# Two transformer blocks on one core: token halves skewed by four weight units at the two joints with a norm over rows

## The chip, the cores and the metric

The kernel runs on one core of one Trainium2 chip. Its engines work side by side, each through its own queue in order: TensorE (PE, matrix products; PEld loads its weights), VectorE (DVE), ScalarE (ACT), GpSimd (POOL) and SyncE (SP, which issues most transfers). They wait for each other by semaphores. The metric is the device time of one execution in microseconds (us); lower is better. All values are 32-bit floating point.

## The reference, cut to what matters

256 tokens of 2048 features pass two blocks. Between the attention and the feed-forward part of the first block, and between the first and the second block, stands a norm over a token's whole row of features, and a second norm follows it at once:

```python
mixed = concat([diff_out, dsa_out]) @ w_o
x = x + gate_a * rms_norm(mixed, g_attn_post)              # joint 1
h = rms_norm(x, g_ffn_pre) * (1.0 + scale_f) + shift_f
ff = (silu(h @ w_gate) * (h @ w_up)) @ w_down
x = x + gate_f * rms_norm(ff, g_ffn_post)                  # joint 2
...
h = rms_norm(x, pre_norm_g)                                # second block
proj = h @ w_in
```

The vectors `gate_a`, `scale_f`, `shift_f`, `gate_f` come from one product of a conditioning vector with `w_ada`, whose weight tiles ("ada" items) are worked off between the other products.

## The kernel before

**Products.** The tokens are two halves of 128, t0 and t1 (t = 0, 1). A weight matrix is worked off in groups (`Grp`) of 512 columns. Its rows come in raw tiles of four chunks of 128 (`kc`), and two chunks make a *unit*. For each unit ScalarE rounds the raw weights to a high part `wh` (line 286) and VectorE subtracts it to get the low part `wl` (L287); both have four buffers. The activations have a high and a low part too (`h2h`, `h2l`, and `h3h`, `h3l`). Each chunk and half takes three products of 128 x 512 into PSUM (`mm`, L65): `wh` by high, `wl` by high, `wh` by low. So a unit is six products for one half.

**Order of the halves.** `Grp.steps()` lays a group out as a list: the first `begin` units for t0, then for t1; the units between for both halves together; the last `end` units for t0, then for t1. So t0's sum is complete `end` units before t1's. With `begin` = 2 the next group can do two units of t0 before it needs anything of t1.

**What sets the order on the engines.** The program is written out by a driver, `run`, that goes through the list of steps with a model of the clock. What follows a product (`post`) is a Python generator: at `yield d` it hands back, and the driver takes it up again when the modelled clock has gone on by d. `mark` and `done` set and ask for names such as `h2.0.0` (half 0, quarter 0). None of this waits on the chip. It decides only in which order instructions stand in the queues.

**Joint 1.** The last group of the attention's output is `wo2_3`. For each half `post_norm_in` (L1142) adds its product to `mo` on VectorE (L1145), squares on ScalarE with a sum (L1146) and multiplies by the gain (L1147). `fin_o(t)` (L1168) goes on: the root of the first norm (VectorE, POOL), then for four quarters of 512 features `resid` (L1155, VectorE: x + norm) and a square on ScalarE (L1178); the second root, put on a diagonal matrix `dg` (L1181). Then, for each quarter, four products of `xr` with `dg` on TensorE transpose and scale at once (`tp`, L65, eight records in the trace); ScalarE adds scale and shift (`hm`, L1192, four instructions); `put_split` (L1158) makes the high part (L1163 on ScalarE, or L1165, a cast on VectorE) and subtracts for the low part (L1166). There are two PSUM buffers for `tp`. `gate0`, the first group of the feed-forward part, uses h2.

**Joint 2.** `down2_3` ends the feed-forward part, `fin_f(t)` (L1261) makes h3 in the same way, with plain transposes (`tp` or `tpb`, L70) of quarters that alternate between ScalarE (L1277) and VectorE (L1273), without a second root: that follows later and is applied after the product. `qa` is the first group of the second block.

Of the kernel before, what the change touches and what calls it, by code (L numbers as in the profile page):

```python
# [39 lines left out]
def kernel(ctx: ExitStack, tc: tile.TileContext, a, freq, out):  # L40
# [32 lines left out]

    # ------------------------------------------------------------------ storage
    slots = deque(range(14))
# [20 lines left out]
    def small(n, name="sm"):  # L96
        t = smp.tile([P, 16], F32, name=name, tag="s")
        return t[:, :n]
# [22 lines left out]

    # ------------------------------------------------------------------ driver
    bg = []
# [250 lines left out]

    # ------------------------------------------------------------------ constants
    v1 = wtile(tag="P", bufs=4, name="v1")
# [129 lines left out]

    # ------------------------------------------------------------------ helpers
    def rstd_of(ssq, n, width, name="rstd"):
# [45 lines left out]

    # ------------------------------------------------------------------ modulation
    def ada_item(load, use, after=lambda: None):
# [162 lines left out]

    # ------------------------------------------------------------------ first norm  # L720
    ssx = cst.tile([P, 2, 4], F32, name="ssx")
# [29 lines left out]

    # ------------------------------------------------------------------ w_in of the first block
    acc = {}
# [43 lines left out]

    # index scores and the selection of keys
    iws = cst.tile([P, 2, 16], F32, name="iws")
# [314 lines left out]

    # ------------------------------------------------------------------ output of the attention
    mix_hi = lambda kc, t: (hid["mh%d" % (kc // 8)][:, kc % 8, t * P:(t + 1) * P],
# [51 lines left out]
    def fin_o(t):  # L1168
        while not done("ada3", "ada4"):
            yield POLL  # L1170
        if "h2" not in hid:
            hid["h2"] = mk_pair("h2")
        yield 0.5
        r = rstd_of(sum4(sso[:, t, :]), 1, D)
        s4 = small(4, "rn4")
        for q in range(4):
            xs = resid(t, q, r, mo, xr)
            A.activation(wtile(name="junk"), xs, AF.Square, accum_out=s4[:, q:q + 1])  # L1178
        r2 = rstd_of(sum4(s4), 1, D)
        dg = wtile(name="dg")[:, :P]  # L1180
        V.tensor_scalar(dg, ident, r2, None, op0=OP.mult)  # L1181
        yield 4.86
        for q in range(4):
            pb = tp_bank()
            for j in range(4):
                k = 4 * q + j
                T.matmul(pb[:, j * P:(j + 1) * P], xr[t][:, k * P:(k + 1) * P], dg, start=True, stop=True,
                         skip_group_check=True)
            m3 = wtile(name="hm").rearrange("p (c q) -> p c q", q=P)
            for j in range(4):  # L1190
                k = 4 * q + j
                A.activation(m3[:, j, :], pb[:, j * P:(j + 1) * P], AF.Identity, scale=Afcol[:, k:k + 1],  # L1192
                             bias=tfcol[:, k:k + 1])
            put_split(hid["h2"], q, t, m3, V)
            mark(f"h2.{t}.{q}")
            yield 3.07
# [5 lines left out]
    for g in range(4):  # L1202
        so2 += Grp(f"wo2_{g}", w_o, 512 * g, 512, range(0, 8), mix_hi,
                   post_norm_in(mo, sso, g, "Ga", fin_o),
                   need=lambda ks, t: ["diff", "ada2"], end=3 if g == 3 else 1).steps()
    steps += [call(mo_alloc)] + merge(so1, scale_f, 1.0)
# [5 lines left out]

    # ------------------------------------------------------------------ feed-forward
    DFF = 5632
# [46 lines left out]
    def fin_f(t):  # L1261
        if "h3" not in hid:
            free_pair("h2")
            hid["h3"] = mk_pair("h3")
        yield 0.5
        r = rstd_of(sum4(ssf[:, t, :]), 1, D)
        xs = [resid(t, q, r, ffacc, xr) for q in range(2)]
        yield 2.33
        for q in range(4):
            pb = quad_transpose(xs[q])  # L1270
            m3 = wtile(name="hm").rearrange("p (c q) -> p c q", q=P)
            if q % 2:
                V.tensor_mul(m3, pb, col1[:, 112 + 4 * q:116 + 4 * q][:, :, None].to_broadcast([P, 4, P]))  # L1273
            else:
                for j in range(4):
                    k = 4 * q + j
                    A.activation(m3[:, j, :], pb[:, j, :], AF.Copy, scale=col1[:, 112 + k:113 + k])  # L1277
            put_split(hid["h3"], q, t, m3, A)
            if q < 2:
                xs.append(resid(t, q + 2, r, ffacc, xr))  # L1280
            mark(f"h3.{t}.{q}")
            yield 1.87
        yield 7.0
        s4 = small(4, "rn4")
        for q in range(4):
            A.activation(wtile(name="junk"), xr[t][:, 512 * q:512 * (q + 1)], AF.Square,
                         accum_out=s4[:, q:q + 1])
        G.tensor_copy(r3[:, t, 0:1], rstd_of(sum4(s4), 1, D))
        V.tensor_scalar(r3[:, t, 1:2], r3[:, t, 0:1], 0.5, None, op0=OP.mult)
        park(t)  # L1290
        mark(f"r3.{t}")
# [7 lines left out]
    for p, (g0, ng) in enumerate(parts):  # L1299
        if p == 0:  # L1300
            fsteps.append(call(after_o))
        fsteps.append(call(act_alloc))
        for g in range(g0, g0 + ng):
            if g == 1:
                fsteps.append(call(rel_mo))
            for nm, w, post in (("gate", w_gate, post_gate(g)), ("up", w_up, post_up(g, g - g0))):
                fsteps += Grp(f"{nm}{g}", w, 512 * g, 512, range(16), lhs2, post,
                              need=lambda ks, t: [f"h2.{t}.{k // 4}" for k in ks],
                              begin=2 if nm + str(g) == "gate0" else 1).steps()
        for g in range(4):  # L1310
            post = post_down(g, p) if p < 2 else post_norm_in(ffacc, ssf, g, "Gf", fin_f)

            def need(ks, t, p=p, g0=g0):
                r = [f"up{k // 4}.{t}" for k in ks]
                return r + (["ada5"] if p == 2 else [])
            fsteps += Grp(f"down{p}_{g}", w_down, 512 * g, 512, range(4 * g0, 4 * (g0 + ng)), lhs_act(p),
                          post, need=need, end=3 if (p, g) == (2, 3) else 1).steps()
    nf = len(fsteps) // 4
# [3 lines left out]

    # ------------------------------------------------------------------ second block
    w_in2 = a["w_in_2"]
# [62 lines left out]

    # gated convolution
    C_IN, B_GATE, C_GATE, Z_CONV = 3136, 5184, 7232, 9280
# [79 lines left out]

    # latent attention  # L1470
    knT, vt, qnT = [None, None], [None, None], [None, None]
# [203 lines left out]

    # output projection
    ot = [None, None]
# [74 lines left out]
```

## Time and profile before

| | |
|---|---|
| runs | 2367.35, 2368.16, 2370.7 us; median 2368.16 |
| span of the profiled execution | 2365.9 us, 27898 instructions |
| TensorE busy | 2315.8 us |
| VectorE, ScalarE, GpSimd busy | 1306.1, 1069.0, 96.8 us |
| mean granted TensorE clock | 0.994 of full speed |
| data moved | 506.57 MB |

The span runs from the first to the last instruction of the one execution that was profiled; the runs are timed whole, without a profile. In a timeline a product's duration reaches past the start of the next, as products overlap: the distance of starts is the pace. Joint 1 lies between 505 and 575 us of the span, joint 2 between 1262 and 1330.

### The profile page before, as it was taken

How to read it: one execution, taken by the hardware profiler on the slowest of the kernel's cores; microseconds unless marked ns; L12 is line 12 of the kernel's file. 1: busy time of each engine (PE TensorE's matmuls, PEld its weight loads, DVE VectorE, ACT ScalarE, POOL GpSimd, SP SyncE). 2: the span in 40 equal slices, each digit the busy share in tenths (PEclk: the TensorE clock that was granted, in tenths of full speed). 3: DMA queues.
4: the chain of work that ended last, by engine and by line, in shares of the span. 5: the costliest groups of instructions: out<-in, count | busy, mean ns of one | idle time of the engine just before them, and what ended most of it. 6: DMA issues, size and time to landing. Idle time of an engine off the chain costs nothing.

```text
span 2365.9 us, 27898 instructions
## 1 busy us (share of the span) xinstructions
PE 2315.8 (98%) x11044; PEld 1842.3 (78%) x11044; DVE 1306.1 (55%) x1710; ACT 1069.0 (45%) x1503; POOL 96.8 (4%) x117
## 2 busy tenths in 40 slices
PE   7999999999999999999998999999999999999998
PEld 5666666677887888888887888888888988888887
DVE  3656756556664444554556655555544654554554
ACT  4434345546444444434444644444445544444443
POOL 1311011010000000000001000000000000000000
PEclk9999999999999999999999999999999999999999
DMA  9996888957775556556554665565565553565563
GB/s 302 330 320 237 318 309 301 318 209 277 242 261 191 191 192 195 179 196 195 186 188 144 220 195 190 179 200 188 179 204 161 168 171 125 172 219 196 187 204 125
DMA packets 237619, 506.57 MB, mean 214 GB/s; under 512 B 9288, under 2 KB 31984, under 8 KB 228400
## 3 DMA queue, kind: packets, MB, share of 16 engines
q1 hardware_dynamic: 235392, 496.14, 62.3%
q0 software_dynamic: 1872, 8.58, 1.1%
q8 instruction: 86, 1.41, 0.2%
q14 instruction: 45, 0.37, 0.0%
q10 hardware_dynamic: 224, 0.07, 0.0%
HBM read 500.56 MB, written 4.19 MB: 213 GB/s over the span
## 4 chain that ended last, share of the span: by engine, by line
PE 75%; DVE 1%; ACT 1%; issue 1%; POOL 0%; DVEq 0%; POOLq 0%; ACTq 0%
PE mm L65 71%; PE tp L70 1%; PE sc L65 1%; PE tp L65 1%; PE tpb L70 1%; DVE wl L287 0%; DVE xr L1155 0%; ACT h3h L1163 0%; DVE h3l L1166 0%; POOL rstd L513 0%; ACT wh L286 0%; ACT junk L1178 0%; DVE ot L1705 0%; ACT hm L1277 0%; DVE hm L1273 0%
## 5 line engine op out<-in xcount | busy, mean ns | idle before, releaser
L287 DVE TENSOR_TENSOR wl<-raw,wh 128x1024 fp32r<-128x1024 f32 (+3 forms) x723 | 871.9, 1212 | 766.5 <-ACT wh L286 760.4
L286 ACT ACTIVATE wh<-raw 128x1024 fp32r<-128x1024 f32 (+3 forms) x723 | 745.9, 1038 | 696.4 <-PE mm L65 686.3
L65 PE MATMUL mm<-wh,h3h 128*128 128x512 f32 (+1 forms) x992 | 387.1, 390 | 1.7 <-ACT h3h L1163 1.2
L65 PE MATMUL mm<-wl,h3h 128*128 128x512 f32 (+1 forms) x992 | 380.7, 384 | 0.4 <-DVE wl L287 0.4
L65 PE MATMUL mm<-wh,h3l 128*128 128x512 f32 (+1 forms) x992 | 381.0, 384 | 0.0
L65 PE MATMUL mm<-wh,h2h 128*128 128x512 f32 x704 | 276.3, 393 | 0.0
L65 PE MATMUL mm<-wl,h2h 128*128 128x512 f32 x704 | 274.6, 390 | 0.9 <-DVE wl L287 0.9
L65 PE MATMUL mm<-wh,h2l 128*128 128x512 f32 x704 | 274.7, 390 | 0.0
L65 PEld LDWEIGHTS mm<-wh,h3h 128*128 128x128 f32 x992 | 186.7, 188 | 37.8 <-ACT h3h L1163 1.6
L65 PEld LDWEIGHTS mm<-wh,h3l 128*128 128x128 f32 x992 | 186.5, 188 | 37.4 <-DVE h3l L1166 0.4
L65 PEld LDWEIGHTS mm<-wl,h3h 128*128 128x128 f32 x992 | 186.8, 188 | 34.8 <-DVE wl L287 0.6
L65 PE MATMUL mm<-wh,h1h 128*128 128x512 f32 (+2 forms) x384 | 154.0, 401 | 3.4 <-ACT wh L286 2.5
L65 PEld LDWEIGHTS mm<-wl,h2h 128*128 128x128 f32 x704 | 132.5, 188 | 28.1 <-DVE wl L287 1.2
L65 PEld LDWEIGHTS mm<-wh,h2h 128*128 128x128 f32 x704 | 132.5, 188 | 27.7 <-issue 0.8
L65 PEld LDWEIGHTS mm<-wh,h2l 128*128 128x128 f32 x704 | 132.4, 188 | 27.6
L65 PE MATMUL mm<-wl,h1h 128*128 128x512 f32 (+2 forms) x384 | 142.7, 372 | 7.8 <-DVE wl L287 7.8
L65 PE MATMUL mm<-wh,h1l 128*128 128x512 f32 (+2 forms) x384 | 142.0, 370 | 1.9 <-DVE h1l L627 1.9
L65 PE MATMUL mm<-wh,acth 128*128 128x512 f32 x352 | 139.3, 396 | 0.0
L65 PE MATMUL mm<-wh,actl 128*128 128x512 f32 x352 | 137.1, 390 | 0.0
L65 PE MATMUL mm<-wl,acth 128*128 128x512 f32 x352 | 137.0, 389 | 0.0
L65 PEld LDWEIGHTS mm<-wh,h1h 128*128 128x128 f32 x384 | 72.8, 190 | 55.7 <-issue 26.7
L65 PEld LDWEIGHTS mm<-wl,h1h 128*128 128x128 f32 x384 | 72.9, 190 | 21.2 <-DVE wl L287 10.9
(412 smaller groups left out, 2777.7 us busy)
## 6 DMA issues: line engine op xcount, KB each, us to landing
raw<-in_w_in_dram SPq DMA_DIRECT2D x134, 1024.0 KB, 5.2
raw<-in_w_ada_dram SPq DMA_DIRECT2D x47, 1024.0 KB, 4.9
raw<-in_w_gate_dram SPq DMA_DIRECT2D x44, 1024.0 KB, 5.3
raw<-in_w_up_dram SPq DMA_DIRECT2D x44, 1024.0 KB, 5.2
raw<-in_w_down_dram SPq DMA_DIRECT2D x44, 1024.0 KB, 5.1
raw<-in_w_ada_dram SPq DMA_DIRECT2D x36, 512.0 KB, 8.9
rawb<-in_w_ada_dram SPq DMA_DIRECT2D x17, 1024.0 KB, 6.5
raw<-in_w_o_conv_dram SPq DMA_DIRECT2D x16, 1024.0 KB, 5.1
```

What stands on the lines that cost most here:

```text
L65: return nc.tensor.matmul(o, l, r, **kw)
L70: return nc.tensor.transpose(o, i, idn)
L286: A.activation(wh[:, :m, :g.n], src, AF.Copy)
L287: V.tensor_sub(wl[:, :m, :g.n], src, wh[:, :m, :g.n])
```

## The change

`wo2_3` and `down2_3` end t0 four units before t1, not three (`wo2_3` also begins with both halves together), and `gate0` begins with four units of t0 in place of two. In `fin_o`, half t1 no longer lets time pass before its first root, and its row is written only after t0's first quarter is done; its four squares are VectorE's (new L1185) in place of ScalarE's; and the high part of h2 is ScalarE's for all quarters but the first of t0. In `fin_f`, t1 passes over the pause too, and t0's quarters 2 and 3 are written after t1's quarters 0 and 1.

```diff
@@ fin_o
-        yield 0.5
+        if t == 0:
+            yield 0.5
         r = rstd_of(sum4(sso[:, t, :]), 1, D)
         s4 = small(4, "rn4")
+        if t == 1:
+            while not done("h2.0.0"):
+                yield 0.3
         for q in range(4):
             xs = resid(t, q, r, mo, xr)
-            A.activation(wtile(name="junk"), xs, AF.Square, accum_out=s4[:, q:q + 1])
+            if t == 0:
+                A.activation(wtile(name="junk"), xs, AF.Square, accum_out=s4[:, q:q + 1])
+            else:
+                V.scalar_tensor_tensor(wtile(name="junk"), xs, 1.0, xs, op0=OP.mult, op1=OP.mult,
+                                       accum_out=s4[:, q:q + 1])
...
-            put_split(hid["h2"], q, t, m3, V)
+            put_split(hid["h2"], q, t, m3, V if t == 0 and q == 0 else A)
@@ wo2 groups
-                   need=lambda ks, t: ["diff", "ada2"], end=3 if g == 3 else 1).steps()
+                   need=lambda ks, t: ["diff", "ada2"], begin=0 if g == 3 else 1,
+                   end=4 if g == 3 else 1).steps()
@@ fin_f
-        yield 0.5
+        if t == 0:
+            yield 0.5
...
         for q in range(4):
+            if t == 0 and q >= 2:
+                while not done(f"h3.1.{q - 2}"):
+                    yield 0.3
@@ gate0
-                              begin=2 if nm + str(g) == "gate0" else 1).steps()
+                              begin=4 if nm + str(g) == "gate0" else 1).steps()
@@ down2_3
-                          post, need=need, end=3 if (p, g) == (2, 3) else 1).steps()
+                          post, need=need, end=4 if (p, g) == (2, 3) else 1).steps()
```

Three places show what moves. The first is VectorE's queue at joint 1, from the add of t1's product (`mo1`) on; `xr1` is t1's row, `dg` the diagonal, `wl` those of gate0's first two units. Before:

```order
L1145 TENSOR_TENSOR mo1_3516<-mm_4451,mo1_3516 128x512
L1147 TENSOR_TENSOR mo1_3516<-mo1_3516,Ga_3521 128x512
L518 TENSOR_REDUCE ssum_4540<-sso_274 128x1
L511 TENSOR_SCALAR rstdv_4542<-ssum_4540 128x1
L1155 SCALAR_TENSOR_TENSOR xr1_4256<-mo1_3516,rstd_4544,xr1_4256 128x512 x4
L518 TENSOR_REDUCE ssum_4559<-rn4_4546 128x1
L511 TENSOR_SCALAR rstdv_4561<-ssum_4559 128x1
L1181 TENSOR_SCALAR dg_4565<-ident_99,rstd_4563 128x128
L1165 CAST h2h0_4480<-hm_4578 128x4x128
L1166 TENSOR_TENSOR h2l0_4482<-hm_4578,h2h0_4480 128x4x128
L287 TENSOR_TENSOR wl_4592<-raw_4589,wh_4591 128x1024
L287 TENSOR_TENSOR wl_4596<-raw_4589,wh_4595 128x1024
```

and of the change:

```order
L1166 TENSOR_TENSOR h2l0_4475<-hm_4552,h2h0_4473 128x4x128
L1155 SCALAR_TENSOR_TENSOR xr1_4256<-mo1_3516,rstd_4537,xr1_4256 128x512
L1185 SCALAR_TENSOR_TENSOR junk_4560,rn4_4539<-xr1_4256 128x512
L1155 SCALAR_TENSOR_TENSOR xr1_4256<-mo1_3516,rstd_4537,xr1_4256 128x512
L1185 SCALAR_TENSOR_TENSOR junk_4563,rn4_4539<-xr1_4256 128x512
L1155 SCALAR_TENSOR_TENSOR xr1_4256<-mo1_3516,rstd_4537,xr1_4256 128x512
L1185 SCALAR_TENSOR_TENSOR junk_4566,rn4_4539<-xr1_4256 128x512
L1155 SCALAR_TENSOR_TENSOR xr1_4256<-mo1_3516,rstd_4537,xr1_4256 128x512
L1185 SCALAR_TENSOR_TENSOR junk_4569,rn4_4539<-xr1_4256 128x512
L518 TENSOR_REDUCE ssum_4571<-rn4_4539 128x1
L511 TENSOR_SCALAR rstdv_4573<-ssum_4571 128x1
L1189 TENSOR_SCALAR dg_4577<-ident_99,rstd_4575 128x128
```

The cast and subtract of t0's first quarter (the subtract is the first row here) move ahead of t1's row, and four squares (L1185) stand between the four resid and behind them, all ahead of `dg`. On TensorE the transpose of t1's first quarter, which reads that `dg`, stands ahead of gate0's first product in both kernels.

The second is ScalarE's queue at joint 1, from the transform of t0's first quarter on (`wh` first of gate0's units 0 and 1, then of unit 2, then of unit 3). Before:

```order
L1192 ACTIVATE hm_4578<-tp_4573,tfcol_130,Afcol_129 128x128 x4
L286 ACTIVATE wh_4591<-raw_4589 128x1024
L286 ACTIVATE wh_4595<-raw_4589 128x1024
L1192 ACTIVATE hm_4618<-tp_4613,tfcol_130,Afcol_129 128x128 x4
L1192 ACTIVATE hm_4630<-tp_4625,tfcol_130,Afcol_129 128x128 x4
L1192 ACTIVATE hm_4657<-tp_4652,tfcol_130,Afcol_129 128x128 x4
L1192 ACTIVATE hm_4669<-tp_4664,tfcol_130,Afcol_129 128x128 x4
L286 ACTIVATE wh_4682<-raw_4599 128x1024
L1192 ACTIVATE hm_4695<-tp_4690,tfcol_130,Afcol_129 128x128 x4
```

and of the change, from `wh` of unit 1 on:

```order
L286 ACTIVATE wh_4595<-raw_4589 128x1024
L1200 ACTIVATE hm_4612<-tp_4607,tfcol_130,Afcol_129 128x128 x4
L1163 ACTIVATE h2h0_4473<-hm_4612 128x4x128
L1200 ACTIVATE hm_4630<-tp_4625,tfcol_130,Afcol_129 128x128 x4
L1163 ACTIVATE h2h0_4473<-hm_4630 128x4x128
L1200 ACTIVATE hm_4654<-tp_4649,tfcol_130,Afcol_129 128x128 x4
L1163 ACTIVATE h2h1_4474<-hm_4654 128x4x128
L1200 ACTIVATE hm_4669<-tp_4664,tfcol_130,Afcol_129 128x128 x4
L1163 ACTIVATE h2h0_4473<-hm_4669 128x4x128
L1200 ACTIVATE hm_4684<-tp_4679,tfcol_130,Afcol_129 128x128 x4
L1163 ACTIVATE h2h1_4474<-hm_4684 128x4x128
L286 ACTIVATE wh_4694<-raw_4599 128x1024
```

Between `wh` of unit 1 and `wh` of unit 2 stood four quarters; now five stand there, each with its cast to the high part (L1163).

The third is VectorE's queue at joint 2; `ffacc1` and `xr1` are t1's, `xr0` t0's, `wl` the low parts of qa's units. Before:

```order
L287 TENSOR_TENSOR wl_9609<-raw_9444,wh_9608 128x1024
L1166 TENSOR_TENSOR h3l0_9586<-hm_9622,h3h0_9584 128x4x128
L1155 SCALAR_TENSOR_TENSOR xr0_4254<-ffacc0_4999,rstd_9595,xr0_4254 128x512
L287 TENSOR_TENSOR wl_9634<-raw_9478,wh_9633 128x1024
L1145 TENSOR_TENSOR ffacc1_5000<-mm_9517,ffacc1_5000 128x512
L1147 TENSOR_TENSOR ffacc1_5000<-ffacc1_5000,Gf_5991 128x512
L1273 TENSOR_TENSOR hm_9650<-tp_9645,col1_113 128x512
L1166 TENSOR_TENSOR h3l0_9586<-hm_9650,h3h0_9584 128x4x128
L1155 SCALAR_TENSOR_TENSOR xr0_4254<-ffacc0_4999,rstd_9595,xr0_4254 128x512
L518 TENSOR_REDUCE ssum_9655<-ssf_275 128x1
L511 TENSOR_SCALAR rstdv_9657<-ssum_9655 128x1
L1155 SCALAR_TENSOR_TENSOR xr1_4256<-ffacc1_5000,rstd_9659,xr1_4256 128x512 x2
```

and of the change:

```order
L1166 TENSOR_TENSOR h3l0_9576<-hm_9610,h3h0_9574 128x4x128
L1155 SCALAR_TENSOR_TENSOR xr0_4254<-ffacc0_5002,rstd_9585,xr0_4254 128x512
L287 TENSOR_TENSOR wl_9622<-raw_9444,wh_9621 128x1024
L1286 TENSOR_TENSOR hm_9635<-tp_9630,col1_113 128x512
L1166 TENSOR_TENSOR h3l0_9576<-hm_9635,h3h0_9574 128x4x128
L1155 SCALAR_TENSOR_TENSOR xr0_4254<-ffacc0_5002,rstd_9585,xr0_4254 128x512
L287 TENSOR_TENSOR wl_9644<-raw_9478,wh_9643 128x1024
L1145 TENSOR_TENSOR ffacc1_5003<-mm_9517,ffacc1_5003 128x512
L1147 TENSOR_TENSOR ffacc1_5003<-ffacc1_5003,Gf_5968 128x512
L518 TENSOR_REDUCE ssum_9651<-ssf_275 128x1
L511 TENSOR_SCALAR rstdv_9653<-ssum_9651 128x1
L1155 SCALAR_TENSOR_TENSOR xr1_4256<-ffacc1_5003,rstd_9655,xr1_4256 128x512 x2
```

The add of t1's product (`ffacc1<-mm`) now stands behind the transform, subtract and third resid of t0 and one more `wl`, where it stood ahead of them.

## Rows read from the trace of the kernel before

**Rows 1.** The page, part 1: busy us of each engine, share of the span, instructions

```profile
PE 2315.8 (98%) x11044; PEld 1842.3 (78%) x11044; DVE 1306.1 (55%) x1710; ACT 1069.0 (45%) x1503; POOL 96.8 (4%) x117
```

**Rows 2.** Windows, 850 to 1262: busy time and instructions by engine, clock, DMA share

```profile
850.00:1262.00 412.00, 412.00 (x1846) 341.18 (x1846) 208.87 (x190) 173.84 (x183) 5.11 (x4) 1.00 0.58 191
```

**Rows 3.** Waits of PE, 500 to 575: instruction, releaser, total, times, longest

```profile
PE tp L65 <- ACT hm L1192: 3.1, 1, 3.1
PE tp L65 <- DVE dg L1181: 2.2, 1, 2.2
PE mm L65 <- DVE wl L287: 0.9, 1, 0.9
```

**Rows 4.** Waits of PE, 1262 to 1330, the same columns

```profile
PE tpb L70 <- DVE xr L1155: 5.4, 2, 4.7
PE mm L65 <- ACT h3h L1163: 1.2, 1, 1.2
PE tp L70 <- DVE xr L1155: 0.8, 1, 0.8
```

**Rows 5.** Windows, 540 to 546, columns as in the second group

```profile
540.00:546.00 6.00, 5.30 (x20) 4.82 (x21) 5.12 (x7) 4.01 (x12) 2.22 (x5) 0.50 0.69 188
```

**Rows 6.** Timeline of PE, joint 1: start, duration, engine, line, operation [idle before]

```profile
526.31 1.92 PE L65 MATMUL ada<-raw,csil 128*32 128x512 f32 x16
530.38 1.16 PE L65 MATMUL tp<-dg,xr 128*128 128x128 f32 x8 [2.15 <-DVE dg L1181]
...
538.42 1.13 PE L65 MATMUL tp<-dg,xr 128*128 128x128 f32 x8 [3.08 <-ACT hm L1192]
...
548.54 1.95 PE L65 MATMUL tp<-dg,xr 128*128 128x128 f32 x16
...
558.76 0.39 PE L65 MATMUL mm<-wh,h2h 128*128 128x512 f32 x1
```

**Rows 7.** Timeline of DVE, joint 1

```profile
518.14 2.10 DVE L287 TENSOR_TENSOR wl<-raw,wh 128x1024 fp32r<-128x1024 f32 x1 [1.76 <-ACT wh L286]
522.34 0.69 DVE L1145 TENSOR_TENSOR mo<-mm,mo 128x512 f32<-128x512 f32 x1 [2.10 <-PE mm L65]
...
530.04 0.28 DVE L1181 TENSOR_SCALAR dg<-ident,rstd 128x128 f32<-128x128 f32 x1 [0.67 <-POOL rstd L513]
530.24 0.68 DVE L1145 TENSOR_TENSOR mo<-mm,mo 128x512 f32<-128x512 f32 x1
...
533.37 2.74 DVE L1155 SCALAR_TENSOR_TENSOR xr<-mo,rstd,xr 128x512 f32<-128x512 f32 x4 [0.65 <-POOL rstd L513]
536.96 0.16 DVE L518 TENSOR_REDUCE ssum<-rn 128x1 f32<-128x4 f32 x1 [0.85 <-ACT junk L1178]
...
538.35 0.43 DVE L1165 CAST h2h<-hm 128x512 fp32r<-128x512 f32 x1
...
539.42 2.35 DVE L287 TENSOR_TENSOR wl<-raw,wh 128x1024 fp32r<-128x1024 f32 x2
```

**Rows 8.** Timeline of ACT, joint 1

```profile
536.84 1.49 ACT L1192 ACTIVATE hm<-tp,tfcol,Afcol 128x128 f32<-128x128 f32 x4
```

**Rows 9.** Line 735, first norm: minimum, median, maximum ns; first and last start

```profile
L735 DVE SCALAR_TENSOR_TENSOR junk<-x x4: 680/684/686, 16.8 to 18.6; 128x512 f32<-128x512 f32 x4
L735 DVE DVE_READ_ACCUMULATOR junk<-x x4: 79/80/81, 17.4 to 19.2; 128x1 f32 x4
```

**Rows 10.** Timeline of ACT, joint 2

```profile
1300.28 1.12 ACT L1277 ACTIVATE hm<-tpb,col 128x128 f32<-128x128 f32 x4
...
1303.42 0.63 ACT L1163 ACTIVATE h3h<-hm 128x512 fp32r<-128x512 f32 x1 [1.36 <-DVE hm L1273]
1303.96 2.94 ACT L286 ACTIVATE wh<-raw 128x1024 fp32r<-128x1024 f32 x3
```

**Rows 11.** Timeline of DVE, joint 2

```profile
1286.25 0.68 DVE L1145 TENSOR_TENSOR ffacc<-mm,ffacc 128x512 f32<-128x512 f32 x1
...
1291.97 1.42 DVE L1155 SCALAR_TENSOR_TENSOR xr<-ffacc,rstd,xr 128x512 f32<-128x512 f32 x2 [0.66 <-POOL rstd L513]
```

## The prediction

> **What bounds the kernel now.** I read the page first: TensorE is busy for 98% of the span [rows 1], so time is won only where TensorE stands still or runs at half clock, and every microsecond added to its row of work is added to the end. A stretch far from the joints has no idle time: 1846 matrix products in 412.00 us, 0.223 us each [rows 2]. So the waits of TensorE around the two joints come next. At joint 1 they are 3.1, 2.2 and 0.9 us [rows 3], 6.2 in all; at joint 2 5.4 (two waits, the longer 4.7), 1.2 and 0.8 [rows 4], 7.4. After the first joint's the clock pays as well: its mean was 0.50, the lower of its two levels (1.2 of 2.4 GHz), over the six microseconds 540 to 546 [rows 5]. Six microseconds at 0.50 do three microseconds' work. All that the change could win back is thus some 6 + 3 us at joint 1 and 7 at joint 2.
>
> The timelines say what is waited for. At joint 1 token half t0 has its last sum added at 522.34 and its diagonal `dg` at 530.04 + 0.28 = 530.32; TensorE transposes at 530.38 [rows 6, 7]. Half t1's `dg` ends at 538.32, and its first quarter is transposed at 538.42, ahead of every product of gate0. The waits list calls that a wait for `hm`, which also ended then, at 536.84 + 1.49 = 538.33 [rows 8]: two releasers at the same instant, so moving ScalarE's work alone wins nothing.
>
> **The change, joint 1.** Times are on the clock of the trace of before.
>
> *t0 earlier.* wo2_3 now ends t0 four units before the group's end instead of three, so one unit of t1 less precedes it: six products, 6 x 0.223 = 1.3 us. But the last low part `wl` ends at 518.14 + 2.10 = 520.24 [rows 7], some 0.5 later than t0's last unit would then want it. So I take 0.9 of 1.3: add at 521.5, `dg` of t0 at 529.5, transposes at once. TensorE meanwhile has 8 instead of 16 ada products (half of 1.92 us [rows 6]) in front of them.
>
> *t1 later.* In the order, VectorE does the cast and subtract of t0's first quarter before t1's row. ScalarE transforms that quarter (1.49 us [rows 8]) after its square for t1, to about 532.7; cast and subtract take 539.42 - 538.35 = 1.07 [rows 7], so t1's row begins at 533.8 (533.37 before). t1's own norm is no limit: add to resid took 533.37 - 530.24 = 3.13 and now ends at 532.6. Before, four resid took 2.74 and ScalarE squared alongside: resid to sum 536.96 - 533.37 = 3.59. Now eight steps stand in one queue, each square reading the resid ahead of it. A resid is 2.74 / 4 = 0.685. A square with accumulation isn't in the joint; the kernel's first norm has the same form at 0.684 plus a read of the accumulator of about 0.08 [rows 9]. Four pairs: 4 x 1.45 = 5.8. Bounds: 3.6, as before, if the squares cost no time of their own, and 6.2, if each of the eight waits a further 0.05 for the one before; I stay near the upper, since both operations stand in one queue and have a duration there. Sum, root and diagonal stay at 538.32 - 536.96 = 1.36. So t1's `dg` ends at 533.8 + 5.8 + 1.4 = 541.0, 2.7 later. TensorE runs out of work about 535.4 (538.42 - 3.08 = 535.34 before; now t0 0.9 earlier and eight ada products more behind it), since the four units of gate0 for t0 stand *behind* this transpose. The wait grows from 3.1 to 5.6.
>
> *ScalarE's queue.* Casts moved from VectorE (0.43 [rows 7]) to ScalarE (0.63, 0.54 start to start [rows 10]). `wh` of gate0's unit 2 now stands behind five quarters with a cast each, where four quarters without one stood ahead of it. From 541.0, at half clock for seven microseconds as before (three products 2 x 0.67 = 1.3; a quarter's transposes, eight records, 0.85 at full clock, which is 1.95 / 2 [rows 6] less its tail, and 1.6 at half): t1 q0 541.1 to 542.7; three products of unit 0 to 544.0; t0 q2 to 545.6; three more to 546.9; t1 q1 to 548.5; full clock from here: unit 1 three to 549.2; t0 q3 to 550.05; three to 550.7. ScalarE follows: t1 q1 548.5 to 550.0 and cast to 550.5; t0 q3 to 552.0, cast to 552.5; `wh` (2.94 / 3 [rows 10], and its latency) to 553.6, VectorE's `wl` (2.35 / 2) to 554.8. TensorE waits 2.9 and 1.0 us. Then t1 q2 is transposed (to 556.2), transformed and cast (558.2), `wh` of unit 3 ends at 559.3, `wl` at 560.4: waits of 2.4 and 0.9. The rest, half of unit 3 and all four units of t1, ends at 567.8. Before, the four units for both halves (48 products) had ended when the fifth unit's first product started at 558.76 [rows 6]. Joint 1: **+9.1**. Bounds: +6, with the squares at 3.6 (2.2 less) and a transform of ScalarE's partly hidden; +13, where the half clock outlasts the new waits.
>
> The Trainium skill (Perfetto Trace Analysis, "Optimizing Scalar/DVE Operations") says that work may be offloaded from VectorE to ScalarE where VectorE is saturated. Here the trace disagrees with the condition, not the rule: VectorE is busy 55% of the span, and the queue that TensorE waits on becomes ScalarE's. [...]
>
> **Joint 2.** t0 ends 1.3 us earlier here too. The wait of 1.2 on `h3h` goes, since t1's last products now lie between. But t1's add, at 1286.25 before [rows 11], is put behind a transform, a subtract, a resid and a `wl` of VectorE's. The `wl` ahead of these ended where that add began, now 1.3 earlier, 1284.9. Then a transform (0.68, the add's shape), ScalarE's cast 0.63, subtract 0.69, resid 0.69, `wl` 1.18: 1288.8. The bare chain from add to resid, 3.13 [rows 7], gives 1291.9, against 1291.97 before [rows 11]. So t1 comes out where it did. TensorE stood there from 1291.97 + 0.7 - 4.7 = 1288.0; without the 1.2 and with a quarter's transposes less ahead (0.4) it is 1286.4: a wait of 6.2 instead of 4.7. Behind it VectorE's new order lets the halves alternate: two resid and a `wl` to 1294.5; subtract of t1 q0, whose cast comes at 1295.4, to 1296.1; resid 1296.8; subtract of t0 q2 to 1298.1; t1 q1 (transform, cast, subtract) to 1300.2; resid 1300.8; t0 q3 to 1302.8. ScalarE transforms t1 q2 behind the cast of t0 q3 (1302.1 + 1.12 + 0.53 [rows 10]), so its subtract ends at 1304.5, the transform of t1 q3 at 1305.2, and t1's last cast stands at 1305.3 instead of 1303.42. `wh` of qa's unit 4 stands directly behind that cast in both kernels [rows 10], so it and its `wl` come 1.9 later. TensorE asked for them without a wait before, so the delay is at most 1.9; less some 0.3 that it then came behind them, joint 2 is **+1.6**. Bounds: -1, where they stay hidden and the lost wait of 1.2 is a gain; +3, where half clock joins the wait of 6.2.
>
> *The rest.* The longer list of steps shifts some ada items; TensorE had no wait there and keeps none: 0. TensorE has no idle time downstream that could absorb a delay [rows 1, 2].
>
> Sum: 9.1 + 1.6 = 10.7; the span becomes 2365.9 + 10.7 = 2376.6. The median of the runs shown, 2368.16, lies 2.3 above the profiled span, so I expect **2379** us.
>
> **The rivals.** 0.2%, 4.7 us, is about what a measurement of this kernel tells from no change.
>
> *Faster (chance 0.06).* The skew does its work: gate0's t0 units fill the time in which t1's norm is made. For: that is 24 products, 5.4 us, against a wait of 3.1. It decides at one point: t1's `dg` would have to be there when TensorE ends t0's second quarter, at 535.4, while t0's subtract alone ends at 533.8 and 7.2 us of steps follow. If it held, joint 1 would win 3.1 + 0.9 and the 3.0 of half clock, joint 2 its small waits, 1.2 + 0.8: 2379 - 10.7 - 9.0, 2359. The skill's sentence in the same section, that breaking up instructions may let work be completed sooner where these engines cause bubbles without being saturated, speaks for it; the alternation of resid and square is such a break-up, yet it serializes on one engine what two did.
>
> *The casts are hidden (0.12).* If `wh` of units 2 and 3 comes in time, the 7.2 us of those four waits go: joint 1 +1.9, joint 2 +1.6, 2371.7, within 0.2%. Against: ScalarE has no free time between t1 q1 and t0 q3.
>
> *The clock stays low through the scattered waits (0.14).* Full-clock work between 548 and 562 is about 4 us; at half it adds 3: 2382. For: six us at 0.50 after a wait of 3.1 [rows 3, 5], and now come 5.6, 2.9 and 2.4. TensorE: Matmul & The Clock Gate, "Part 1: The HAM clock gate", says that the default is the throttled state and activity releases it; that fits the row and leaves this open.
>
> *Only part of the serial cost shows (0.08).* The short price of squares and an early ScalarE: +6 in all, 2374.
>
> **How the numbers follow.** My own sum has the remaining 0.60. Slower by over 0.2%: 0.60 + 0.14 + 0.08 = 0.82; same 0.12; faster 0.06. The range runs from 2371, which leaves out the faster case and some of the hidden casts, to 2386: joint 1 at +13 and joint 2 at +3 with 2 us to spare; about 0.17 lies outside.
>
> **What would show it.** Right: TensorE waits 5 to 6 us for `dg` ahead of t1 q0; two new waits for `wh` of some 2.5 us each with 1 us for `wl` behind them; at joint 2 one wait of 6 to 6.6 for `xr`, none of 1.2, and some 2 at unit 4 of qa. Wrong: t1's eight steps below 4 us; a wait for `dg` under 3 us; no waits for `wh`; or a stall outside the joints, for a raw weight tile or behind an adacc step that waits for its own tile.

## The result: 14 us slower, nearly all of it at the first joint

| | before | after |
|---|---|---|
| median of four runs each (us) | 2368.83 | 2382.45 |
| lowest to highest | 2367.35 to 2370.7 | 2381.98 to 2384.16 |
| span of the profiled execution | 2365.9 | 2380.3 |

The ratio is 1.0063, with a 95% interval of 1.005 to 1.0076: slower. The forecast was 2379, in a range of 2371 to 2386.

The page of after, part 1, first row, beside [rows 1]: TensorE is busy 4.6 us longer for the same 11044 instructions, and 9.8 us of the 14.4 us of span are new idle time.

```profile
PE 2320.4 (97%) x11044; PEld 1843.3 (77%) x11044; DVE 1305.9 (55%) x1711; ACT 1070.8 (45%) x1502; POOL 96.6 (4%) x117
```

TensorE's waits in the trace of after, first from 500 to 590 us (joint 1), then from 1262 to 1350 (joint 2): instruction, releaser, total, times, longest.

```profile
PE tp L65 <- ACT wh L286: 5.1, 1, 5.1
PE mm L65 <- ACT wh L286: 5.1, 2, 3.2
PE tp L65 <- DVE dg L1189: 1.7, 1, 1.7
PE mm L65 <- DVE wl L287: 1.4, 3, 0.5
...
PE tp L70 <- DVE xr L1155: 6.2, 1, 6.2
PE mm L65 <- DVE wl L287: 1.4, 3, 0.8
PE mm L65 <- ACT wh L286: 1.1, 1, 1.1
PE tpb L70 <- DVE xr L1155: 0.6, 1, 0.6
```

Joint 1 waits for 13.3 us in all where it waited 6.2 [rows 3]. Joint 2 waits for 9.3; in before the list of joint 2 has one row more than the three of [rows 4], so it waited 7.8 there, not the 7.4 that the prediction adds up:

```profile
PE mm L65 <- DVE wl L287: 0.4, 1, 0.4
```

Two waits for `wh` are new at joint 1: the weights of gate0's units 2 and 3. The timeline of TensorE, after, joint 1, says where they stand:

```profile
528.66 1.16 PE L65 MATMUL tp<-dg,xr 128*128 128x128 f32 x8 [1.66 <-DVE dg L1189]
...
539.71 2.05 PE L65 MATMUL tp<-dg,xr 128*128 128x128 f32 x8 [5.10 <-ACT wh L286]
...
552.08 0.80 PE L65 MATMUL mm<-wh,h2h 128*128 128x512 f32 x1 [3.17 <-ACT wh L286]
553.34 0.80 PE L65 MATMUL mm<-wl,h2h 128*128 128x512 f32 x1 [0.46 <-DVE wl L287]
...
554.35 1.91 PE L65 MATMUL tp<-dg,xr 128*128 128x128 f32 x8
...
559.47 0.79 PE L65 MATMUL mm<-wh,h2h 128*128 128x512 f32 x1 [1.93 <-ACT wh L286]
560.73 0.80 PE L65 MATMUL mm<-wl,h2h 128*128 128x512 f32 x1 [0.47 <-DVE wl L287]
```

The start distances show the rest: behind 560.73 the next products start at 561.33 and 561.75, 0.4 to 0.6 us apart, where at full clock it is 0.223 [rows 2]. Windows of after (length, TensorE busy with instructions, granted clock, DMA share, GB/s), beside [rows 5]:

```profile
539.00:546.00 7.00, 6.29 (x26) 0.55 0.53 168
546.00:552.00 6.00, 2.90 (x20) 1.00 1.03 377
552.00:565.00 13.00, 10.07 (x27) 0.50 0.51 176
```

At joint 1 of before the clock was low once, after the wait for `dg`. Now it is at its lower level a second time, for 13 us, behind the first wait for `wh`. At 0.50, 10.07 us of work are 5.0 us lost. So joint 1 is accounted for by 13.3 - 6.2 = 7.1 of waits and 5.0 of clock, 12.1 together. The product that starts the fifth unit of gate0 stood at 558.76 [rows 6] and stands at 570.68: +11.9, and the trace of after had run 1.2 us ahead before the joint (the same product starts at 439.73 and at 440.89). So the joint costs some 13, of which about 1 is left without a name.

VectorE and ScalarE of after show who releases what. VectorE first: t1's serial resid and square (start of the first pair, end of the last), its `dg`.

```profile
532.54 0.75 DVE L1155 SCALAR_TENSOR_TENSOR xr<-mo,rstd,xr 128x512 f32<-128x512 f32 x1
...
538.14 0.08 DVE L1185 DVE_READ_ACCUMULATOR junk<-xr 128x1 f32 x1
...
539.33 0.29 DVE L1189 TENSOR_SCALAR dg<-ident,rstd 128x128 f32<-128x128 f32 x1 [0.72 <-POOL rstd L513]
```

And ScalarE, from `wh` of units 0 and 1 to that of units 2 and 3:

```profile
538.49 2.00 ACT L286 ACTIVATE wh<-raw 128x1024 fp32r<-128x1024 f32 x2 [7.06 <-DMA raw<-in_w_gate_dram]
540.39 1.49 ACT L1200 ACTIVATE hm<-tp,tfcol,Afcol 128x128 f32<-128x128 f32 x4
...
550.45 0.63 ACT L1163 ACTIVATE h2h<-hm 128x512 fp32r<-128x512 f32 x1
550.99 1.04 ACT L286 ACTIVATE wh<-raw 128x1024 fp32r<-128x1024 f32 x1
556.31 1.51 ACT L1200 ACTIVATE hm<-tp,tfcol,Afcol 128x128 f32<-128x128 f32 x4 [4.28 <-PE tp L65]
...
558.38 1.04 ACT L286 ACTIVATE wh<-raw 128x1024 fp32r<-128x1024 f32 x1
```

The wait of 5.1 is named for `wh`, but ends with `dg`, at 539.33 + 0.29 = 539.62. `wh` of unit 2 stands directly behind the fifth quarter's cast. The row at 556.31 is the one to remember: ScalarE itself stood still for 4.28 us, for a transpose that on TensorE stands *behind* unit 2's products (554.35). TensorE waits for ScalarE's `wh` of unit 2, ScalarE then for TensorE's transposes, and TensorE for `wh` of unit 3, which stands behind those transforms.

Joint 2, after: the add of t1's product and its resid on VectorE, then the last cast of h3 and `wh` on ScalarE, beside [rows 10, 11].

```profile
1301.27 0.68 DVE L1145 TENSOR_TENSOR ffacc<-mm,ffacc 128x512 f32<-128x512 f32 x1
...
1304.35 1.41 DVE L1155 SCALAR_TENSOR_TENSOR xr<-ffacc,rstd,xr 128x512 f32<-128x512 f32 x2 [0.66 <-POOL rstd L513]
...
1318.01 0.63 ACT L1163 ACTIVATE h3h<-hm 128x512 fp32r<-128x512 f32 x1 [1.36 <-DVE hm L1286]
1318.54 2.94 ACT L286 ACTIVATE wh<-raw 128x1024 fp32r<-128x1024 f32 x3
```

t1's resid is 12.4 later than before, about what joint 1 had lost (+11.9), so t1 comes out where it did; `wh` of qa is 1318.54 - 1303.96 = 14.6 later, so 2.2 come behind the resid, where VectorE now alternates between the halves.

### The profile page after: what moved, and what is told of

The parts are those of the page before. It is cut to its first block, busy times and chain, and to the rows that moved or that the text cites. A ratio compares the mean times of both kernels' runs of the same rounds, so it can differ in the third digit from the quotient of the medians.

```text
span 2380.3 us, 27899 instructions
## 1 busy us (share of the span) xinstructions
PE 2320.4 (97%) x11044; PEld 1843.3 (77%) x11044; DVE 1305.9 (55%) x1711; ACT 1070.8 (45%) x1502; POOL 96.6 (4%) x117
## 4 chain that ended last, share of the span: by engine, by line
PE 93%; DVE 3%; ACT 2%; DMA 1%; issue 1%; POOL 0%; SPq 0%; ACTq 0%; DVEq 0%; POOLq 0%
PE mm L65 84%; PE ada L65 3%; PE sc L65 2%; PE tp L70 2%; PE tp L65 2%; DVE wl L287 1%; ACT wh L286 1%; PE tpb L70 1%; DMA ada<-in_w_ada_dram 0%; DMA raw<-in_w_ada_dram 0%; DMA raw<-in_w_gate_dram 0%; ACT hm L1200 0%; DMA v<-in_g_ffn_pre_dram 0%; DVE xr L1155 0%; ACT h3h L1163 0%
```

## The experiments

The theory was the prediction's: TensorE's wait for `dg` and late weights at joint 1, with ScalarE's casts and VectorE's squares in the queues ahead. The rivals that the runs had to tell apart: it is the casts; the squares; the demand for units 2 and 3 ahead of t1's products, whatever the steps do; the landing of the raw weight tiles; the low clock. Times are medians, each beside that of the kernel before, measured together with it on the same chip, with the ratio and its interval. After was measured beside another set of runs of before, so where a run is compared with after, the two differences from before are compared; that of after is 13.6.

**One joint alone.** The change at joint 1 only, then at joint 2 only.

`j1_only` is after with `fin_f` and `down2_3` as before, `j2_only` before with these two as after:

```diff
@@ j2_only, against before: fin_f and down2_3
+            if t == 0 and q >= 2:
+                while not done(f"h3.1.{q - 2}"):
+                    yield 0.3
...
-                          post, need=need, end=3 if (p, g) == (2, 3) else 1).steps()
+                          post, need=need, end=4 if (p, g) == (2, 3) else 1).steps()
```

> The change at joint 1 alone. Theory A, two separate losses (joint 1 some 12.5 us, joint 2 1.8 us, as the shifts between the two traces suggest): 12 to 13 us over the kernel before, and TensorE's waits at joint 1 as in the changed kernel (5.1 before t1's first transposes, 3.2 and 1.9 for the high parts of units 2 and 3). Rival, the joints are coupled by when weight tiles are loaded: under 10 or over 15 us.

> The change at joint 2 alone. Theory A: 1.8 us over the kernel before (within what can be told from no change), waits at joint 2 of 6.2 for t1's row and 1.1 and 0.8 at unit 4 of qa. Rival, joint 2 by itself is a gain that joint 1 spoils: 2 us or more under the kernel before.

Joint 1 alone 2382.15 beside 2367.75, ratio 1.0058 [1.0045, 1.0071]: +14.4, where 12 to 13 were expected, with the waits of after (5.1 for `dg`, 3.0 and 1.9 for `wh`). Joint 2 alone 2369.67 beside 2367.75, 1.0006 [0.9997, 1.0015]; its trace has the wait of 6.2 and the 1.1 for `wh`. The loss is joint 1's.

**The casts back on VectorE.**

```diff
@@ a_casts_dve, against after
-            put_split(hid["h2"], q, t, m3, V if t == 0 and q == 0 else A)
+            put_split(hid["h2"], q, t, m3, V)
```

> The changed kernel with the high part of h2 cast on VectorE for all quarters again, all else as changed. Theory A, ScalarE's casts ahead of the high parts of units 2 and 3 make the two late waits and with them the second stretch of half clock: 5 casts of 0.54 less ahead of unit 2, the wait of 3.2 falls below 1, the clock stays up, 5 to 8 us under the changed kernel. Rival B, the raw weight tile of units 2 and 3 isn't there earlier: the waits stay near 3.2 and 1.9 and the time within 2 us of the changed kernel.

2380.32 beside 2367.75, 1.0052 [1.0038, 1.0065]: +12.6, 1.0 less than after (2.1 by the bare medians), which the intervals don't separate. TensorE's waits for `wh` at joint 1 in this trace:

```profile
PE mm L65 <- ACT wh L286: 3.2, 2, 1.8
```

They fall from 5.1 to 3.2 and don't go. `wh` of unit 2 still stands directly behind a transform (it starts at 549.79).

**The squares of t1 back on ScalarE.**

```diff
@@ a_squares_act, against after
-            if t == 0:
-                A.activation(wtile(name="junk"), xs, AF.Square, accum_out=s4[:, q:q + 1])
-            else:
-                V.scalar_tensor_tensor(wtile(name="junk"), xs, 1.0, xs, op0=OP.mult, op1=OP.mult,
-                                       accum_out=s4[:, q:q + 1])
+            A.activation(wtile(name="junk"), xs, AF.Square, accum_out=s4[:, q:q + 1])
```

> The changed kernel with t1's four squares on ScalarE again, all else as changed. Theory A, the serial row on VectorE costs 2.0 us of the wait ahead of t1's first transposes: dg 2.0 us earlier (537.6), the wait 3.1 instead of 5.1, 2 us under the changed kernel. Rival C, the raw tile of gate0's first two units lands at 538.5 whatever the norm does, and holds ScalarE's queue: dg comes earlier but the first product of gate0 does not, under 1 us gained.

2383.51 beside 2367.75, 1.0064 [1.0051, 1.0077]: +15.8, nothing won. `dg` on VectorE and `wh` of units 0 and 1 on ScalarE in this trace:

```profile
537.05 0.29 DVE L1185 TENSOR_SCALAR dg<-ident,rstd 128x128 f32<-128x128 f32 x1 [0.72 <-POOL rstd L513]
```
```profile
538.14 2.00 ACT L286 ACTIVATE wh<-raw 128x1024 fp32r<-128x1024 f32 x2 [2.18 <-DMA raw<-in_w_gate_dram]
```

`dg` is 2.3 us earlier (537.34 against 539.62), and the wait ahead of t1's transpose falls from 5.1 to 3.0. But ScalarE stands still until gate0's first raw tile lands, about 538.1; `wh` starts only 0.35 earlier than in after (538.49), and so do the quarters behind it. What the serial squares cost lies under the landing of that tile.

**gate0 begins with two units of t0, as before; the rest of the change stays.**

```diff
@@ a_begin2, against after
-                              begin=4 if nm + str(g) == "gate0" else 1).steps()
+                              begin=2 if nm + str(g) == "gate0" else 1).steps()
```

> The changed kernel with gate0 beginning with two units of t0 again, all else as changed. Theory D, new: the raw tile of gate0's units 2 and 3 lands at 547.9 whatever the norm does, since its load waits until the first tile's two low parts are made, and four units of t0 ahead of t1's first products demand it too early. Then TensorE has 12 products of t1 (2.7 us) to do in the first late wait and 12 more ahead of unit 3: the waits of 3.2 and 1.9 fall below 1 each, the second stretch at half clock goes, 6 to 9 us under the changed kernel. Rival A, the norm's longer row and the casts are the loss: within 2 us of the changed kernel.

2371.64 beside 2368.22, 1.0018 [1.0009, 1.0026]: +3.4, 10.2 us less than after (10.8 by the bare medians). Its waits at joint 1, and `wh` of unit 2:

```profile
PE tp L65 <- ACT wh L286: 5.1, 1, 5.1
PE tp L65 <- DVE dg L1189: 1.6, 1, 1.6
PE mm L65 <- DVE wl L287: 1.2, 2, 0.8
```
```profile
551.80 1.04 ACT L286 ACTIVATE wh<-raw 128x1024 fp32r<-128x1024 f32 x1
```
```profile
552.00:565.00 13.00, 12.05 (x55) 1.00 0.74 258
```

The wait of 5.1 is still there, casts and squares are where the change put them, and `wh` of unit 2 starts at 551.80, in after at 550.99 (counted from t0's first transpose 0.5 earlier than in after). But no product waits for `wh` any more: TensorE asks for it later, as twelve products of t1 on units 0 and 1 lie in between. The clock is at 1.00 from 552 to 565 here (last row).

**begin = 4 alone, and begin = 3 alone, in the kernel before.**

```diff
@@ b_begin4 (and b_begin3, with 3), against before
-                              begin=2 if nm + str(g) == "gate0" else 1).steps()
+                              begin=4 if nm + str(g) == "gate0" else 1).steps()
```

> The kernel before with one part of the change alone: gate0 begins with four units of t0 instead of two. Theory E: demanding units 2 and 3 for t0 ahead of t1's products of units 0 and 1 is the loss by itself, whatever the casts, the squares and the skew do: waits for the high parts of units 2 and 3 of 1.5 to 3 us each with half clock behind them, 6 to 10 us over the kernel before. Rival A: without the casts on ScalarE the high parts come in time, as the sum of the forecast has it: under 3 us over.

> The kernel before with one number changed: gate0 begins with three units of t0 in place of two (four cost +10.8 us). Theory (each unit that t0 asks for ahead of t1's products costs its own late weights, and the waits and the half clock add up by unit): only unit 2 is asked for early, one wait of about 2 us for wh and one of 0.9 for wl are left where four units had two of each, and the time rises by 4 to 6 us. Rival (the first late unit is the whole price, since ScalarE catches up once it is past the quarters): the same 9 to 11 us as with four. Second rival (the second unit is the price, unit 2 is nearly in time): within 2 us of before.

Four: 2378.33 beside 2367.57, 1.0043 [1.003, 1.0057], +10.8 by one number, with every cast of h2 on VectorE and every square on ScalarE. Three: 2369.72 beside 2367.12, 1.0013 [1.0004, 1.0022], +2.6. TensorE, then ScalarE, in the trace with four:

```profile
549.43 0.50 PE L65 MATMUL mm<-wh,h2h 128*128 128x512 f32 x1 [2.08 <-ACT wh L286]
...
551.34 3.49 PE L65 MATMUL tp<-dg,xr 128*128 128x128 f32 x16
...
557.41 0.49 PE L65 MATMUL mm<-wh,h2h 128*128 128x512 f32 x1 [1.90 <-ACT wh L286]
```
```profile
548.32 1.06 ACT L286 ACTIVATE wh<-raw 128x1024 fp32r<-128x1024 f32 x1 [0.28 <-DMA raw<-in_w_gate_dram]
553.33 3.08 ACT L1192 ACTIVATE hm<-tp,tfcol,Afcol 128x128 f32<-128x128 f32 x8 [3.96 <-PE tp L65]
556.29 1.06 ACT L286 ACTIVATE wh<-raw 128x1024 fp32r<-128x1024 f32 x1
```

The ring of after again: `wh`, products, transposes, transforms, `wh`, 8.0 us from one `wh` to the next (548.32 to 556.29), in which TensorE has six products of t0 and the transposes of two quarters (sixteen records). With three the wait for unit 2 is there too, and TensorE then has t1's products, while ScalarE does its transforms. TensorE and ScalarE in the trace with three:

```profile
548.93 0.50 PE L65 MATMUL mm<-wh,h2h 128*128 128x512 f32 x1 [1.19 <-ACT wh L286]
...
561.06 0.39 PE L65 MATMUL mm<-wh,h2h 128*128 128x512 f32 x1
```
```profile
554.78 1.09 ACT L286 ACTIVATE wh<-raw 128x1024 fp32r<-128x1024 f32 x1
```

`wh` of unit 3 comes at 554.78, and TensorE doesn't wait for it. The row at 561.06 is the fifth unit's first product, 2.3 later than in before (558.76 [rows 6]). Windows from 550 to 565, columns as in those of after, with three and with four: the clock is 1.00 and 0.66.

```profile
550.00:565.00 15.00, 14.70 (x77) 1.00 0.69 239
550.00:565.00 15.00, 11.53 (x41) 0.66 0.59 209
```

So the case that the first late unit is the whole price fell. The time lies between the two others (4 to 6, and within 2), and its interval, 0.9 to 5.2 us, reaches both; the traces decide for unequal units: three add 2.0 us of waits (8.2 against 6.2) and no second stretch of low clock, four 5.6 (11.8) and that stretch. By the medians unit 2 costs 2.6, and unit 3, which closes the ring, 10.8 - 2.6 = 8.2.

**Earlier raw tiles.** Two ada items fewer ahead of gate0, so that its first raw tile is issued and lands over 5 us earlier; in after, and in before with only the skew of `wo2_3`.

```diff
@@ a_ada4 (against after) and sk_ada4 (against before, with begin=0 and end=4 in wo2_3)
-    steps += gate_f[:6] + merge(fsteps[:nf], gate_f[6:], 0.9)
+    steps += gate_f[:4] + merge(fsteps[:nf], gate_f[4:], 0.9)
```

> The changed kernel with four instead of six ada items between the two groups (the other two later), so that gate0's two raw tiles are loaded some 5 us earlier; four units of t0 first as changed. Theory D: the tiles land by 533 and 538, ScalarE isn't held, the late waits fall below 1 each although t1's dg comes up to 2.4 us later (two low parts stand ahead of its row): 4 to 8 us under the changed kernel. Rival A, norm and casts: the late waits stay, within 2 us or slower.

> The kernel before with wo2_3 alone skewed by four units and four instead of six ada items ahead of gate0; squares, casts, gate0's two units and joint 2 as before. Theory D says that gate0's weights come early enough for three products of unit 0 ahead of t1's transposes: TensorE's wait for t1's dg falls from 3.1 to 2 or less, 2 to 4 us under the kernel before. Rival: the two low parts ahead of t1's row delay its dg by 2.4 and take it all back, within 1.5 us of the kernel before.

a_ada4 2383.22 beside 2368.22, 1.0065 [1.0052, 1.0078]: +15.0, nothing won; sk_ada4 2371.94, 1.0017 [1.0008, 1.0026]: slower by 3.7, which neither of the expected cases had (its wait ahead of t1's transpose is 5.4, and one of 2.7 for h2's high part is new). VectorE in a_ada4:

```profile
534.02 2.36 DVE L287 TENSOR_TENSOR wl<-raw,wh 128x1024 fp32r<-128x1024 f32 x2 [2.23 <-ACT wh L286]
...
544.21 0.29 DVE L1189 TENSOR_SCALAR dg<-ident,rstd 128x128 f32<-128x128 f32 x1 [0.72 <-POOL rstd L513]
```

The tile is there at 532.9, and the driver now writes its two `wl` ahead of t0's cast and t1's row: VectorE waits 2.23 us for `wh`, and `dg` comes 4.9 later than in after (4.1 counted from t0's `dg`). The wait ahead of t1's transpose grows to 6.1, and one of 2.4 for h2's high part is new. The ring itself is cut here: ScalarE makes `wh` of units 2 and 3 in one go, from 553.80 on, and one wait for `wh`, of 2.5, is left of two. Early weights in the same queue as the norm cost what they save.

**The clock.** Products that nothing reads, put into the waits: in after, 12 and 9 ahead of t0's units 2 and 3; in before, 13 and 19 ahead of t1's first transpose at joints 1 and 2.

```diff
@@ a_warm, against after, ahead of t0's products of unit 2 (12) and 3 (9)
+                for _ in range(12 if u["kcs"][0] == 4 else 9):
+                    nc.tensor.matmul(g.ps[1], warm["l"], warm["r"], start=True, stop=True, skip_group_check=True)
...
@@ b_warm, against before, ahead of t1's quarters in fin_o (13) and fin_f (19)
+        if t == 1:
+            idle_products(13)
...
```

> The changed kernel with 12 and 9 idle products (128x512, into a sum that is begun afresh later) in the two late waits ahead of units 2 and 3, so that TensorE is not idle there. If the second stretch at half clock (552 to 565) is the part that the forecast lacked: granted clock 1.00 there, 3 to 5 us under the changed kernel although work is added. Rival: what TensorE waits for is late anyway, at most 1 us gained, whatever the clock.

> The kernel before with idle products (13 of 0.23 us at joint 1, 19 at joint 2, into a free sum bank) ahead of t1's first transposes, so that TensorE is not idle there. If the half clock behind a wait costs what the windows say (3.0 and 2 us), the granted clock stays 1.00 through both joints and the kernel is 3 to 5 us faster than before, and than the changed one by 17. Rival: the chains on VectorE and ScalarE set the pace behind the waits, not TensorE's clock: within 1.5 us of the kernel before.

a_warm 2379.65 beside 2368.22, 1.0051 [1.0038, 1.0063]: +11.4, 2.2 less than after (2.8 by the bare medians), the intervals overlapping. b_warm 2366.99 beside 2367.57, 0.9994 [0.9985, 1.0003]: the same. Windows, columns as above, a_warm and then b_warm, with a row of its timeline of TensorE:

```profile
552.00:565.00 13.00, 10.54 (x52) 1.00 0.64 220
```
```profile
540.00:546.00 6.00, 5.38 (x31) 1.00 0.65 187
1285.00:1293.00 8.00, 7.38 (x42) 1.00 0.01 2
1301.00:1303.00 2.00, 2.00 (x6) 0.50 0.00 0
```
```profile
1299.70 0.63 PE L70 MATMUL tp<-ident,xr 128*128 128x128 f32 x4 [1.94 <-DVE xr L1161]
```

In the windows that the idle products were meant for the clock is at its higher level, where it was 0.50 in after (552 to 565) and in before (540 to 546 [rows 5], and 1293 to 1297). In b_warm that brought the fifth unit's first product from 558.76 to 557.01, 1.6 of the 3.0 that six us at 0.50 seemed to be worth (the run was 0.1 ahead). At joint 2 the idle products fill the wait of 4.7; the others for `xr`, 0.7 and 0.8 before [rows 4], are 1.7 and 1.9 in its list: TensorE at full clock meets VectorE's and ScalarE's chains sooner. Behind the wait of 1.94 the clock falls to 0.50 after all. Up to that wait's end b_warm was 2.2 us ahead of before (this transpose starts at 1299.70 and at 1301.91), behind the low stretch only 0.6 (qa's first transposes at 1320.70 and 1321.31), which is what the medians show. So b_warm doesn't say what a full clock through both joints is worth: the low stretch of joint 2 was moved, not removed.

**The skew alone.** `wo2_3` skewed and t1's row put behind t0's first quarter; gate0, squares, casts and joint 2 as before.

```diff
@@ c_min, against before
+        if t == 1:
+            while not done("h2.0.0"):
+                yield 0.3
...
-                   need=lambda ks, t: ["diff", "ada2"], end=3 if g == 3 else 1).steps()
+                   need=lambda ks, t: ["diff", "ada2"], begin=0 if g == 3 else 1,
+                   end=4 if g == 3 else 1).steps()
```

> The changed kernel with gate0's two units, casts on VectorE, squares on ScalarE and joint 2 as before: of the change only the skew of wo2_3 and the order of t1's row behind t0's first quarter remain. Theory E: what is left neither wins nor loses, since gate0's first raw tile lands at 538.5 either way: within 2 us of the kernel before. Rival: t0's earlier end is a gain that the other parts hid: 2 us or more under it.

2368.7 beside 2367.57, 1.0005 [0.9996, 1.0013]: the same. Its wait ahead of t1's transpose is 3.0, as before (3.1 [rows 3]): the skew shortened neither that wait nor the time.

None of these kernels is clearly faster than before.

## Why the prediction was right, and where a size was off

*The sign and its mechanism* were right: new waits for `wh` of units 2 and 3, late behind ScalarE's quarters. But the edit that decides is `begin`, which the prediction didn't price by itself: alone it costs 10.8, undone it gives back 10.2, and all the other edits together cost the 3.4 that are left in a_begin2, about half of it at joint 2.

*t0 earlier.* Its transposes start 1.7 earlier [rows 6], of which about 1 is the trace's lead. That leaves some 0.6, against 0.9; the half us that `wl` was to take appears as a wait of 0.49. Nothing came of it at the end (c_min).

*t1 later.* Its four pairs took 538.22 - 532.54 = 5.7, forecast 5.8. `dg` ended at 539.62, not 541.0, 1.3 behind before's 538.32 or 2.4 with the lead, against 2.7; the wait was 5.1 for 5.6. So the term was right, and without effect: a_squares_act took 2.3 of it away and won nothing, because ScalarE couldn't begin `wh` before 538.1. The prediction had no term for that landing. Nor does the alternation of resid and square break up an instruction, as its rival "faster" has it: before had the same four of each, the squares on ScalarE, and took 3.6 for them where one queue takes 5.7.

*ScalarE's queue.* `wh` of unit 2 ended at 552.0 (forecast 553.6) and that of unit 3 at 559.4 (559.3). The four waits are 3.17, 0.46, 1.93 and 0.47, 6.0 in all against 2.9, 1.0, 2.4 and 0.9, 7.2. Only part of them is the casts': without these 5.1 for `wh` becomes 3.2. b_begin4 has 4.0 without one cast on ScalarE. So the rival by which hidden casts would give all 7.2 back was rightly held small. Its paragraph gives another reason (no free time on ScalarE); the one that the runs show, the ring through TensorE's own transposes, stands in the forecast's walk from unit 2 to unit 3, without a price of its own. The Trainium skill (Perfetto Trace Analysis, "Optimizing Scalar/DVE Operations") has offloading from VectorE to ScalarE make sense where VectorE is saturated. It was 55% busy here, and taking the casts back made the kernel 1.0 us faster beside its own before, which is not clear of the measurement.

*The term that was mis-sized* is the clock of joint 1, "full clock from here" behind 548.5. It was full for 3.5 us, most of it a wait, and then at 0.50 from 552 to 565: 5.0 us instead of none. The waits came out smaller than forecast, the four by 1.2 and that for `dg` by 0.5. Joint 1 comes to 12 or 13 in place of 9.1, near its upper bound, which had been worded so ("where the half clock outlasts the new waits"). That is the rival "the clock stays low", priced at +3 and 2382; it had 0.14. a_warm shows that the clock can be kept up, and gives 2.2 to 2.8 of the 5.0 back, not clear of the measurement.

*What the change could win* was put at 6 + 3 us at joint 1. The 3 of half clock were too much: with the clock at 1.00 at joint 1, b_warm's trace wins 1.6 there, and 0.6 is left at the end, which can't be told from nothing. By its trace part of the low clock lies beside chains that TensorE waits for anyway. That takes some of the 9.0 that the rival "faster" was worth (2359), and the skew of `wo2_3` by itself left the wait ahead of t1's transpose at 3.0 (c_min).

*Joint 2.* Forecast +1.6: a wait of 6.2, none of 1.2, `wh` 1.9 later. Measured: a wait of 6.2, none for `h3h`, `wh` 2.2 later, waits 1.5 longer in all (9.3 against 7.8), and +1.9 [-0.7, 3.6] by the run with joint 2 alone.

*The sum.* 10.7 was forecast; the spans differ by 14.4 and the medians by 13.6. About 3 of the difference is joint 1: 5.0 of clock, less the 1.7 by which the waits came out smaller. That these two errors have opposite signs is luck.

What stays open: a_casts_dve, a_warm and after differ by less than their intervals, so the shares of the casts and of the clock rest on the traces. That `wh` of unit 2, made ready in time, would save begin = 4 wasn't tried by itself. In after its raw tile is issued at 541.96, when VectorE is done with the `wl` of the first tile (539.57 + 2.36 = 541.93), and in b_begin4 ScalarE waited 0.28 for it even so; a_ada4 has it earlier, but pays for that at the norm.

## What to carry to other kernels

Giving one half more units to run ahead fills a gap only if those units' weights are ready by then; otherwise it asks for them earlier and moves the work that would have covered their preparation behind them. Before widening a skew, follow one whole ring through the in-order queues (weights, products, transposes, transforms, weights) and compare its length with the work that TensorE has inside it: in b_begin4 8.0 us against six products and the transposes of two quarters. And try the numbers of a schedule one at a time: three units cost 2.6 us, four 10.8.

## What the runs showed of the hardware

- The granted clock was at 0.50 for 13 us (552 to 565) in which TensorE was busy for 10.07, after a wait of 3.17 and with further ones of 0.46, 1.93 and 0.47; it was back at 1.00 from 566 to 570, behind products without a wait from 560.73 on. In before it came back after six (540 to 546). The Trainium skill (TensorE: Matmul & The Clock Gate, "Part 1: The HAM clock gate") calls the throttled state the default and has activity release it. The trace agrees in that the clock came back behind products without a wait; the 5.0 us of work between 552 and 559.4, broken by waits, did not bring it back.
- Products that nothing reads, put into one wait at each joint of before, kept the clock at 1.00 where two stretches at 0.50 had been seen, of six us at joint 1 and of four at joint 2 (1293 to 1297). At joint 1 the trace gains 1.6 us. At joint 2 the clock fell to 0.50 later (1301 to 1303), behind a wait of 1.94, and 0.6 us is left of both (0.9985 to 1.0003, so at most 3.6 and perhaps nothing).
- The waits list put 5.1 us down to `wh`, while `dg` ended 0.09 us before the transpose started. a_squares_act settles it: there `dg` ends at 537.34, the transpose starts at 537.44, and `wh` only begins at 538.14.
